# A decoder block on one core: the split weights of both feed-forwards and of four projections each at their own place modulo 128 bytes

## The chip, the core and the metric

The kernel runs on one core of a Trainium2 chip. The metric is device time in microseconds for one execution; the times below are medians over several executions. "PE" is TensorE's matmul, "PEld" its weight load, "DVE" VectorE, "ACT" ScalarE, "POOL" GpSimd, "SP" SyncE, whose queue issues most loads. One partition of the on-chip memory holds a row of bytes; all 128 partitions of a tile start at the same byte. Places below are that start byte modulo 128.

## The reference

Two layers on 512 tokens of width 1024, all in float32. Layer 0 has a dilated attention mixer, layer 1 an mLSTM mixer; behind each mixer stands a SwiGLU feed-forward with 2816 hidden units.

```python
def swiglu(xn, w_in, w_out):
    gu = xn @ w_in
    return (jax.nn.silu(gu[..., :D_FF]) * gu[..., D_FF:]) @ w_out

h = x
for i in range(2):
    if i == 0:
        h = h + dilated_attention_mixer(rms_norm(h, attn_norm[0]), positions, attn_w_in[0], attn_w_out[0])
    else:
        h = h + mlstm_mixer(rms_norm(h, mlstm_norm[0]), mlstm_w_in[0], ...)
    h = h + swiglu(rms_norm(h, ffn_norm[i]), ffn_w_in[i], ffn_w_out[i])
return rms_norm(h, final_norm)
```

## The kernel before

Every large product is done as three matmuls on float32r operands. A float32 operand is split into a high part, which ScalarE copies out in float32r, and a low part, the difference, which VectorE forms. `SPLITS` (line 46) then takes high by high, high by low and low by high, all summed in one PSUM bank. So each pair of 128-row pieces costs three matmuls, and each matmul has its own 128 by 128 weight load (the operand that stays in the array) and its own stream (the operand that moves, 512 or 256 columns).

`split_chunk` (line 231) makes the two parts of a weight chunk: a high and a low tile of 128 by 1024 float32r from the pool "w" (`wp`), each with three buffers used in turn. Four 128-row pieces of a chunk serve 12 matmuls for each of two groups of 128 outputs, thus 24 matmuls per chunk.

The stages, in the order of the program, with the matmuls that the change touches:

- Attention, up to 429 us: products at lines 541, 1059 and 1343 and projections at lines 275 and 360. Their weights come through `split_chunk` too.
- `awo`, the output projection of the attention, eight chunks through `multiply` (line 275), stream 512 wide. One of its chunks lies in a spare pool.
- Feed-forward 0 (`ffn_in`, line 1508): eight plain chunks `f0j0`, `f0j2` (line 275, 512 wide), then nine steps of seven products (a Strassen-Winograd scheme over halves of the tokens and of the width), line 1681, 24 matmuls each, 256 wide. The weight chunks are named `f0j4A11`, `f0j4S1` and so on. The stream is the split activations in tiles `op0` to `op13` of the pool "ffn0". Then the output products at line 1996, whose weights are named `f0P1_0w` and so on.
- mLSTM: `mqk` and `mo` (line 275, 512 wide), `mv` (lines 329 and 360), the heads, and the output projection `mwo` (line 275).
- Feed-forward 1 as feed-forward 0, with the pool "ffn1": plain chunks `f1j0`, `f1j2`, 63 products at line 1681, and the output products at line 2411 and 2533, in which the activations (`f1P`, in "ffn1") are what stays in the array and the weights are what moves.

The places are set by the order in which pools are opened and by the sizes of their tiles (lines 88 to 107):

```python
xp = pool(ctx, "act")
gap0 = pool(ctx, "gap0")
wp = pool(ctx, "w")
gap1 = pool(ctx, "gap1")
gap0.tile([P, 16], F32, name="gap0")
gap1.tile([P, 112], F32, name="gap1")
```

`gap0` puts 64 bytes ahead of the weights. All tiles of "w" then start at byte 96 modulo 128; the activation tiles in "act" and the operand tiles of "ffn0" and "ffn1" start at 32. A piece of a tile (256 columns, 128 weights) starts a multiple of 128 bytes further on. So in the chunks at lines 275, 1059, 1681 and 1996 the weights stand at 96 and the stream at 32, 64 bytes apart, and at lines 329, 360, 1343 and 2411 it is the other way round (stays at 32, moves at 96).

The tile framework orders the instructions by the dependencies of the buffers; nothing of that order depends on an address.

Of the kernel before, what the change touches and what calls it, by code (L numbers as in the profile page):

```python
# [3 lines left out]

# [7 lines left out]
F32 = mybir.dt.float32  # L12
F32R = mybir.dt.float32r
# [4 lines left out]
P = 128  # L18
# [3 lines left out]
KC = D // P  # L22
# [20 lines left out]
           (19, 20, 21))  # L43
LAST_OUTPUTS = {6: 22, 7: 23}
W_BUFS = 3
SPLITS = [(0, 0), (0, 1), (1, 0)]


# [27 lines left out]
def tile_hybrid_dilated_attn_mlstm(  # L76
# [8 lines left out]
    def pool(stack, name, **kw):  # L85
        return stack.enter_context(tc.tile_pool(name=name, bufs=1, **kw))

    cp = pool(ctx, "const")
    xp = pool(ctx, "act")
    gap0 = pool(ctx, "gap0")  # L90
    wp = pool(ctx, "w")
    gap1 = pool(ctx, "gap1")
    ps = pool(ctx, "psum", space=bass.MemoryType.PSUM)


# [7 lines left out]
    ones_r = cp.tile([P, P], F32R, name="ones_r")  # L103
    nc.vector.tensor_copy(ones_r, ones.to_broadcast([P, P]))

    gap0.tile([P, 16], F32, name="gap0")
    gap1.tile([P, 112], F32, name="gap1")
    idle_w = xp.tile([P, 2, SEQ], F32R, tag="x%d" % (KC - 1), name="idle_w")[:, 0]
    nc.vector.tensor_copy(idle_w, ones.to_broadcast([P, SEQ]))
    idle_ps = ps.tile([P, 512], F32, tag="t", name="idle", bufs=1)  # L110
# [94 lines left out]
    def load_chunk(src, shape, name):  # L205
        n = int(np.prod(shape[1:]))
        view = lambda t: t[:, :n].rearrange("p (a b) -> p a b", a=shape[1])
        raw = wp.tile([P, 1024], F32, tag="wraw", name=name + "_w", bufs=W_BUFS)
        nc.sync.dma_start(view(raw), src)
# [5 lines left out]
    def behind_scores():  # L215
        return tc.issue_after(ahead_of_splits[0]) if ahead_of_splits[0] is not None else nullcontext()
# [3 lines left out]
    def behind_factors():  # L220
        return tc.issue_after(ahead_of_casts[0]) if ahead_of_casts[0] is not None else nullcontext()
# [4 lines left out]
    def run_late(_):  # L226
        while lows:
            with tc.issue_after(last_on(mybir.EngineType.DVE)):
                lows.pop(0)()

    def split_chunk(chunk):

        raw, n, view, name = chunk
        p, more, bufs = (spare[0], "4", 1) if spare and next(splits) % (W_BUFS + 1) == W_BUFS else (wp, "", W_BUFS)
        hi = p.tile([P, 1024], F32R, tag="whi" + more, name=name + "_h", bufs=bufs)
        lo = p.tile([P, 1024], F32R, tag="wlo" + more, name=name + "_l", bufs=bufs)
        with behind_factors():
            nc.scalar.activation(hi[:, :n], raw[:, :n], AF.Copy)  # L238
        def low():
            nc.vector.tensor_tensor(lo[:, :n], raw[:, :n], hi[:, :n].bitcast(F32), op=ALU.subtract)  # L240
        if late[0]:
            lows.append(low)
        else:
            with behind_scores():
                low()
        return view(hi), view(lo)
# [23 lines left out]
    def multiply(acc, whl, pairs, ch, m, nk, ks=None):  # L270

        for k in ks or range(min(4, nk - 4 * ch)):
            kk = 4 * ch + k
            for a, b in SPLITS:
                nc.tensor.matmul(  # L275
                    acc, whl[a][:, k, m * P:(m + 1) * P], pairs[b][kk],
                    start=(kk == 0 and (a, b) == SPLITS[0]),
                    stop=(kk == nk - 1 and (a, b) == SPLITS[-1]))

# [39 lines left out]
    def project_tokens(pairs, w2d, c0, evac, name, tok=lambda t, tb: t[:, tb * P:(tb + 1) * P]):  # L319

        acc = [acc_tile("%s_%d" % (name, m)) for m in range(2)]
        for ch in range(KC // 4):
            whl = split_chunk(weight_chunk(w2d, ch, c0, 4, "%s_k%d" % (name, ch)))
            for m in range(2):
                with fenced():
                    for i, k in itertools.product(range(2), range(4)):
                        kk = ch * 4 + k
                        for a, b in SPLITS:
                            nc.tensor.matmul(
                                acc[m][:, i * 256:(i + 1) * 256],  # L330
                                tok(pairs[a][kk], 2 * m + i), whl[b][:, k, :],
                                start=(kk == 0 and i == 0 and (a, b) == SPLITS[0]),
                                stop=(kk == KC - 1 and (a, b) == SPLITS[-1]),
                                skip_group_check=True)
# [5 lines left out]
    def wide_chunk(parts, ch, name):  # L340
        w = 512 // len(parts)
        raw = wp.tile([P, 1024], F32, tag="wraw", name="%s_k%d_w" % (name, ch), bufs=W_BUFS)
        for i, part in enumerate(parts):
# [80 lines left out]
    with ExitStack() as actx:  # L424
# [22 lines left out]
        ang, n, sn, cs = (tmp[:, 0, i * P:(i + 1) * P] for i in range(4))  # L447
# [36 lines left out]
        xtok = ap.tile([P, TB, D], F32, tag="heads", name="x_tok")  # L484
        raws = [wp.tile([P, 1024], F32, tag="wraw", name="first%d_w" % i, bufs=W_BUFS) for i in range(2)]
        piece = lambda t, q: t[q // 2][:, (q % 2) * 512:(q % 2 + 1) * 512]
# [32 lines left out]
            else:  # L519
                nc.scalar.activation(h[k], xps[k], AF.Copy)  # L520

        his = [wp.tile([P, 1024], F32R, tag="whi", name="first%d_h" % i, bufs=W_BUFS) for i in range(2)]
        los = [wp.tile([P, 1024], F32R, tag="wlo", name="first%d_l" % i, bufs=W_BUFS) for i in range(2)]
        facc = [ps.tile([P, 512], F32, tag="o", name="a0g0q_%d" % m, bufs=2) for m in range(2)]

        def v12_parts(pr):
# [953 lines left out]
    def norm(key, k0, name, ssum=None, wait=1):  # L1480
        pair = x_tiles(name)
        add = None
        if ssum is None:
            ssum, add = squares_of(name)
        for k in range(KC):
            split_act(pair[0][k], pair[1][k], h[k], col(key, k0 + k))
            if add is not None:
                add(k)
        v = npl.tile([P, TB], F32, tag="rs_v4", name=name + "v", bufs=2)
        box = {}  # L1490

        def sums():
            sp = ps.tile([P, 512], F32, tag="t", name=name + "ss", bufs=1)
            for tb in range(TB):
                nc.tensor.matmul(sp[:, tb:tb + 1], ssum[:, tb * P:(tb + 1) * P], ones[:, 0:1],
                                 start=True, stop=True)
            nc.vector.tensor_copy(v, sp[:, :TB])
            box["finish"]()
        rbc, r, hook = inverse_rms(v, name, box)
        defer(wait, sums)  # L1500
        return pair, rbc, r, hook
# [3 lines left out]
    PLAIN = 4  # L1505
# [249 lines left out]
    def output_products(layer, fp, wo, sums_of_rows):  # L1755
# [17 lines left out]
        def subtract(out, x, y):  # L1773
            nc.vector.tensor_tensor(out, x, y, op=ALU.subtract)

        def split_operand(name, u, src):

            i = UNITS * (PARTS.index(name) % 3) + u
            nm = "f%d%s_%d" % (layer, name, u)
            if i < 2 * len(PRODUCTS):  # L1780
                t = fp.tile([P, 2, 2, HALF], F32R, tag="op%d" % i, name=nm)
                hi, lo = t[:, 0], t[:, 1]
            else:
                hi, lo = [fp.tile([P, 2, HALF], F32R, tag="gu0", name=nm, bufs=3) for _ in range(2)]
            nc.scalar.activation(hi, src, AF.Copy)
            subtract(lo, src, hi.bitcast(F32))
            ops[name, u] = [[t[:, k] for k in range(2)] for t in (hi, lo)]
# [18 lines left out]
        def prepare_first_sum(u, own, nm):  # L1806

            view = lambda t: t.rearrange("p (k n) -> p k n", k=2)
            hi = wp.tile([P, 1024], F32R, tag="whi", name=nm + "_h", bufs=W_BUFS)
            lo = wp.tile([P, 1024], F32R, tag="wlo", name=nm + "_l", bufs=W_BUFS)  # L1810
            for t, ks in first_sums[u]:
                nc.scalar.activation(view(hi)[:, ks], t, AF.Copy)
                subtract(view(lo)[:, ks], t, view(hi)[:, ks].bitcast(F32))
            whl["P5", u] = view(hi), view(lo)
            for t, ks in first_sums[u]:
                subtract(view(own)[:, ks], t, view(own)[:, ks])
            split_operand("P5", u, sums[u])
# [125 lines left out]
        first, second = (0, 1) if sums_of_rows else (1, 0)  # L1943
# [6 lines left out]
        for e in order:  # L1950
            name, i = e.split("_")
# [29 lines left out]
    pair, rbc, _, hook = norm("ffn", 0, "n1", ssum)  # L1981
    with ExitStack() as fctx:
        fp = pool(fctx, "ffn0")
# [60 lines left out]
    with ExitStack() as mctx:  # L2044
# [56 lines left out]
        gacc = acc_tile("gates")  # L2101

        def gates():
            gh = wp.tile([P, KC, P], F32R, tag="whi", name="gates_h", bufs=W_BUFS)
            nc.gpsimd.memset(gh.bitcast(F32), 0.0)
            for o in range(2):
                s = slice(32 * o, 32 * o + H)
                w = graw[:, :, o * H:(o + 1) * H]
                nc.scalar.activation(gh[:, :, s], w, AF.Copy)
                nc.vector.tensor_tensor(gh[:, :, 64 + 32 * o:64 + 32 * o + H], w, gh[:, :, s].bitcast(F32),  # L2110
                                        op=ALU.subtract)
            for k in range(KC):
                for b_ in range(2):
                    nc.tensor.matmul(gacc, gh[:, k, :], pair[b_][k], start=(k == 0 and b_ == 0),
                                     stop=(k == KC - 1 and b_ == 1))
# [68 lines left out]
        i = 0  # L2184
# [165 lines left out]
    pair, rbc, _, hook = norm("ffn", KC, "n3", ssum)  # L2350
    with ExitStack() as fctx:
        fp = pool(fctx, "ffn1")
        dp = pool(fctx, "scratch1", space=bass.MemoryType.DRAM)
        R = 32
        hid, operands, prepare, work = output_products(1, fp, ffn_w_out[1], False)
# [116 lines left out]
        def newton(tb):  # L2472
            v, r, a2 = fv[:, tb:tb + 1], fr[:, tb:tb + 1], fa[:, tb:tb + 1]
            nc.vector.reciprocal(r, r)
            nc.vector.tensor_scalar(a2, r, v, r, op0=ALU.mult, op1=ALU.mult)
            nc.vector.scalar_tensor_tensor(r, a2, -3.0, r, op0=ALU.add, op1=ALU.mult)
            return r
# [45 lines left out]
        for acc, tb, cs in tiles:  # L2523
# [21 lines left out]
            r = newton(tb)  # L2545
# [29 lines left out]
```

## Time and profile before

| | us |
|---|---|
| median of the runs before | 1357.64 (1357.39 to 1357.9, two runs) |
| the profiled execution, its own time | 1358.57 |
| its span, first to last instruction | 1356.8 |
| PE busy | 1340.1 |
| DVE busy | 1133.0 |
| ACT busy | 813.3 |
| the 63 products of feed-forward 0 (line 1681) | 171.38 |
| the 63 products of feed-forward 1 (line 1681) | 171.38 |
| the 420 matmuls of feed-forward 1's output at line 2411 | 95.97 |

A row of the chain of waits reads: start in us, length in us, engine, output, line, number of instructions. A length divided by the number of matmuls is the pace from one start to the next. That is what counts here: a single matmul's duration is longer than the pace, since consecutive matmuls overlap. A row of the windows reads: stretch, its length, busy time and count by engine, granted clock of TensorE, DMA share, GB/s; a window with a line's filter counts the instructions of that line alone.

### The profile page before, as it was taken

What the parts mean: (1) busy time and instruction counts of PE and PEld (TensorE: products, weight loads), DVE (VectorE), ACT (ScalarE), POOL (GpSimd) and SP (SyncE); (2) the same over time, 40 slices, a digit from 0 to 9 for tenths busy, and PEclk for the clock granted to TensorE, in tenths of its full rate; (3) what the DMA queues carried; (4) which work ended last, traced back from release to release, by engine and by line L of the source; (5) the groups of instructions that cost most, each with busy time, mean ns of one, the idle gap of its engine ahead of it and who ended that gap; (6) DMA issues with size and microseconds to landing.
All of it is one profiled execution on the core that took longest, in us unless ns stands there. A gap on an engine that the chain in (4) does not pass through costs nothing.

```text
span 1356.8 us, 23343 instructions
## 1 busy us (share of the span) xinstructions
PE 1340.1 (99%) x9100; PEld 1222.1 (90%) x9100; DVE 1133.0 (84%) x1787; ACT 813.3 (60%) x1303; POOL 196.7 (14%) x272
## 2 busy tenths in 40 slices
PE   9999999999999999999999999999999999999997
PEld 7898899999988888999999998898878899999886
DVE  7988789899876389888888898898848988997887
ACT  6676577667674255555577464795534555558854
POOL 3000013141412001000010110122200112112113
PEclk9999999999999999999999999999999999999999
DMA  9354244554676357343362743324333545447863
GB/s 306 122 181 155 79 141 143 169 172 155 184 261 191 125 142 172 114 125 125 125 156 79 171 126 87 100 63 124 94 118 97 127 133 172 141 136 173 189 171 101
DMA packets 141270, 194.90 MB, mean 144 GB/s; under 512 B 9028, under 2 KB 106116, under 8 KB 141160
## 3 DMA queue, kind: packets, MB, share of 16 engines
q1 hardware_dynamic: 120128, 140.73, 33.0%
q0 software_dynamic: 19808, 52.48, 16.1%
q8 instruction: 71, 1.16, 0.3%
q10 hardware_dynamic: 1224, 0.21, 0.1%
q14 instruction: 39, 0.32, 0.1%
HBM read 167.30 MB, written 22.54 MB: 140 GB/s over the span
## 4 chain that ended last, share of the span: by engine, by line
PE 79%; DVE 10%; ACT 3%; issue 3%; DMA 1%; POOL 0%; SPq 0%; ACTq 0%; DVEq 0%; POOLq 0%
PE fo L1996 7%; PE f1j_u L1681 5%; PE f0j_u L1681 5%; PE f1j_c L1681 4%; PE f0j_c L1681 4%; PE f1j_p L1681 4%; PE f0j_p L1681 4%; PE mwo L275 3%; PE f1j L275 3%; PE f0j L275 3%; PE mqk L275 3%; PE awo L275 3%; PE finp L2411 3%; PE mo L275 3%; PE finc L2411 2%
## 5 line engine op out<-in xcount | busy, mean ns | idle before, releaser
L1803 POOL DMA_DIRECT2D f0S<-in_ffn_w_out_dram x10 | 8.7, 874 | 248.9 <-DVE f0hid L1720 162.3
L2364 POOL DMA_DIRECT2D hD<-hB x32 | 20.7, 655 | 109.6 <-DVE hB L2361 109.4
L1828 POOL DMA_DIRECT2D f1T<-in_ffn_w_out_dram x15 | 17.8, 1186 | 86.1 <-ACT f1T L1831 40.8
L240 DVE TENSOR_TENSOR v1P_l<-v1W,v1P_h 128x1024 fp32r<-128x1024 f32 x14 | 17.1, 1224 | 10.3 <-ACT v1P_h L238 10.3
L275 PE MATMUL mo<-n_h,mo_k_h 128*128 128x512 f32 x64 | 25.7, 401 | 0.0
L275 PE MATMUL mwo<-yo_h,mwo_k_h 128*128 128x512 f32 x64 | 25.5, 398 | 0.0
L275 PE MATMUL awo<-ao_h,awo_k_h 128*128 128x512 f32 x64 | 25.5, 398 | 0.0
L275 PE MATMUL mwo<-yo_l,mwo_k_h 128*128 128x512 f32 x64 | 25.5, 398 | 0.0
L275 PE MATMUL mwo<-yo_h,mwo_k_l 128*128 128x512 f32 x64 | 25.5, 398 | 0.0
L275 PE MATMUL mo<-n_h,mo_k_l 128*128 128x512 f32 x64 | 25.4, 397 | 0.0
L275 PE MATMUL mqk<-n_h,mqk_k_h 128*128 128x512 f32 x64 | 25.4, 397 | 0.0
L275 PE MATMUL mo<-n_l,mo_k_h 128*128 128x512 f32 x64 | 25.4, 396 | 0.0
L275 PE MATMUL mqk<-n_l,mqk_k_h 128*128 128x512 f32 x64 | 25.3, 396 | 0.0
L275 PE MATMUL awo<-ao_l,awo_k_h 128*128 128x512 f32 x64 | 25.3, 396 | 0.0
L275 PE MATMUL f0j<-n_h,f0j_h 128*128 128x512 f32 x64 | 25.3, 395 | 0.0
L275 PE MATMUL f1j<-n_h,f1j_h 128*128 128x512 f32 x64 | 25.3, 395 | 0.0
L275 PE MATMUL awo<-ao_h,awo_k_l 128*128 128x512 f32 x64 | 25.3, 395 | 0.0
L275 PE MATMUL mqk<-n_h,mqk_k_l 128*128 128x512 f32 x64 | 25.2, 394 | 0.0
L275 PE MATMUL f0j<-n_l,f0j_h 128*128 128x512 f32 x64 | 25.2, 394 | 0.0
L275 PE MATMUL f1j<-n_l,f1j_h 128*128 128x512 f32 x64 | 25.2, 394 | 0.0
L275 PE MATMUL f0j<-n_h,f0j_l 128*128 128x512 f32 x64 | 25.2, 394 | 0.0
L275 PE MATMUL f1j<-n_h,f1j_l 128*128 128x512 f32 x64 | 25.2, 394 | 0.0
(2746 smaller groups left out, 5999.6 us busy)
## 6 DMA issues: line engine op xcount, KB each, us to landing
f0j_w<-in_ffn_w_in_dram SPq DMA_DIRECT2D x17, 512.0 KB, 5.7
f1j_w<-in_ffn_w_in_dram SPq DMA_DIRECT2D x17, 512.0 KB, 6.9
f1T<-in_ffn_w_out_dram POOLq DMA_DIRECT2D x15, 512.0 KB, 6.4
f0hid<-in_ffn_w_in_dram SPq DMA_DIRECT2D x9, 512.0 KB, 6.1
f1hid<-in_ffn_w_in_dram SPq DMA_DIRECT2D x9, 512.0 KB, 5.0
v0W<-in_attn_w_in_dram SPq DMA_DIRECT2D x8, 512.0 KB, 6.8
v1W<-in_attn_w_in_dram SPq DMA_DIRECT2D x8, 512.0 KB, 3.7
awo_k_w<-in_attn_w_out_dram SPq DMA_DIRECT2D x8, 512.0 KB, 4.7
```

The source lines that it names most:

```text
L240: nc.vector.tensor_tensor(lo[:, :n], raw[:, :n], hi[:, :n].bitcast(F32), op=ALU.subtract)
L275: nc.tensor.matmul(acc, whl[a][:, k, m * P:(m + 1) * P], pairs[b][kk], start=(kk == 0 and (a, b) == SPLITS[0]), stop=(kk == nk - 1 and (a, ...
L1681: nc.tensor.matmul(acc[name][:, m * HALF:(m + 1) * HALF], whl[a][:, k, m * P:(m + 1) * P], ops[okey][b][:, k], start=(fresh and m == 0 and ...
L1803: nc.gpsimd.dma_start(t, src[1][:, ks], accum_op=ALU.add)
L1828: nc.gpsimd.dma_start(view(to), weight_rows(hk * UNITS + u, n), accum_op=ALU.add)
L1996: nc.tensor.matmul(acc, w[a_][:, k, m * P:(m + 1) * P], b[b_][k], start=(fresh and k == 0 and (a_, b_) == SPLITS[0]), stop=(k == 1 and (a_ ...
L2364: nc.gpsimd.dma_start(hD[k // 4].rearrange("(b i) x -> i b x", i=R)[:, :, c0:c0 + R], t[R * a_:R * (a_ + 1)])
L2411: nc.tensor.matmul(acc[m], a[a_][k][:, (2 * t + m) * P:(2 * t + m + 1) * P], w[b_][:, k, :], start=(fresh and k == 0 and (a_, b_) == SPLIT ...
```

## The change

The two gap pools go. The high and low tiles of "w" become 1056 columns wide (`PAD` is 32 columns, 128 bytes) and only 1024 of them are used, from a column that `place_of` gives by the chunk's name. The pool "w" now begins at byte 32, so column 16, which most names get, is byte 96 as before. For the products' weights of both feed-forwards the column goes up by 5 (20 bytes) from chunk to chunk, modulo 32; for the plain chunks by 10 (40 bytes); for `awo`, `mqk`, `mo` and `mwo` by 5. Over a feed-forward's 63 products every multiple of 4 bytes is used once or twice. A tile of 32 bytes ahead of the others in "ffn1" moves everything in that pool from 32 to 64 modulo 128: the stream of feed-forward 1's products, and the staying operand of line 2411.

Both high and low tile of a chunk get the same column, so a place holds for 24 matmuls. On every engine the instructions, their shapes and their waits stand in the same order as before; only addresses differ. The weights at lines 541, 1059, 1343, 329, 360 and 1996 keep byte 96; raw tiles of "w", which SP's queue fills, go from 96 to 32.

```diff
+PAD = 32
...
-    gap0 = pool(ctx, "gap0")
     wp = pool(ctx, "w")
-    gap1 = pool(ctx, "gap1")
...
+    products = ("A11", "S1", "S2", "A12", "S3", "S4", "A22")
+
+    def place_of(name):
+
+        i, found = None, re.match(r"f([01])j(\d+)([AS]\d+)$", name)
+        if found:
+            i = int(found[1]) * 66 + (int(found[2]) - PLAIN) // 2 * 7 + products.index(found[3])
+            return (i * 5 - 8) % PAD
+        found = re.match(r"f([01])j(\d)_(\d)(\d)$", name)
+        if found:
+            i = int(found[1]) * 8 + int(found[2]) * 2 + int(found[3]) * 2 + int(found[4])
+            return (i * 10 - 8) % PAD
+        found = re.match(r"(awo|mqk|mo|mwo)(\d)_k(\d)$", name)
+        if found:
+            i = ("awo", "mqk", "mo", "mwo").index(found[1]) * 8 + int(found[3]) * 4 + int(found[2])
+            return (i * 5 - 8) % PAD
+        return 16
+
     def split_chunk(chunk):
 
         raw, n, view, name = chunk
         p, more, bufs = (spare[0], "4", 1) if spare and next(splits) % (W_BUFS + 1) == W_BUFS else (wp, "", W_BUFS)
-        hi = p.tile([P, 1024], F32R, tag="whi" + more, name=name + "_h", bufs=bufs)
-        lo = p.tile([P, 1024], F32R, tag="wlo" + more, name=name + "_l", bufs=bufs)
+        at, pad = (0, 0) if more else (place_of(name), PAD)
+        hi = p.tile([P, 1024 + pad], F32R, tag="whi" + more, name=name + "_h", bufs=bufs)[:, at:at + 1024]
+        lo = p.tile([P, 1024 + pad], F32R, tag="wlo" + more, name=name + "_l", bufs=bufs)[:, at:at + 1024]
...
         fp = pool(fctx, "ffn1")
+        fp.tile([P, 8], F32, name="gap3")
```

The three other places that take tiles of "w" (the first projection, the first sums of feed-forward 0's output, the gates) get 1056 columns and column 16.

More of the change, by code (lines that the diff above doesn't have):

```diff
@@ L2 @@
 import math
+import re
 from contextlib import ExitStack, nullcontext
@@ L104, in tile_hybrid_dilated_attn_mlstm @@
     nc.vector.tensor_copy(ones_r, ones.to_broadcast([P, P]))
-    gap0.tile([P, 16], F32, name="gap0")
-    gap1.tile([P, 112], F32, name="gap1")
     idle_w = xp.tile([P, 2, SEQ], F32R, tag="x%d" % (KC - 1), name="idle_w")[:, 0]
@@ L520, in x_keep @@
                 nc.scalar.activation(h[k], xps[k], AF.Copy)
-        his = [wp.tile([P, 1024], F32R, tag="whi", name="first%d_h" % i, bufs=W_BUFS) for i in range(2)]
-        los = [wp.tile([P, 1024], F32R, tag="wlo", name="first%d_l" % i, bufs=W_BUFS) for i in range(2)]
+        his = [wp.tile([P, 1024 + PAD], F32R, tag="whi", name="first%d_h" % i, bufs=W_BUFS)[:, 16:1040] for i in range(2)]
+        los = [wp.tile([P, 1024 + PAD], F32R, tag="wlo", name="first%d_l" % i, bufs=W_BUFS)[:, 16:1040] for i in range(2)]
         facc = [ps.tile([P, 512], F32, tag="o", name="a0g0q_%d" % m, bufs=2) for m in range(2)]
@@ L1808, in prepare_first_sum @@
             view = lambda t: t.rearrange("p (k n) -> p k n", k=2)
-            hi = wp.tile([P, 1024], F32R, tag="whi", name=nm + "_h", bufs=W_BUFS)
-            lo = wp.tile([P, 1024], F32R, tag="wlo", name=nm + "_l", bufs=W_BUFS)
+            hi = wp.tile([P, 1024 + PAD], F32R, tag="whi", name=nm + "_h", bufs=W_BUFS)[:, 16:1040]
+            lo = wp.tile([P, 1024 + PAD], F32R, tag="wlo", name=nm + "_l", bufs=W_BUFS)[:, 16:1040]
             for t, ks in first_sums[u]:
@@ L2103, in gates @@
         def gates():
-            gh = wp.tile([P, KC, P], F32R, tag="whi", name="gates_h", bufs=W_BUFS)
+            gh = wp.tile([P, 1024 + PAD], F32R, tag="whi", name="gates_h", bufs=W_BUFS)[:, 16:1040]
+            gh = gh.rearrange("p (k n) -> p k n", k=KC)
             nc.gpsimd.memset(gh.bitcast(F32), 0.0)
```

## The prediction

> **What bounds the kernel now.** I read the page first, for its busy times and the clock.
>
> ```profile
> span 1356.8 us, 23343 instructions
> PE 1340.1 (99%) x9100; PEld 1222.1 (90%) x9100; DVE 1133.0 (84%) x1787; ACT 813.3 (60%) x1303; POOL 196.7 (14%) x272
> PEclk9999999999999999999999999999999999999999
> PE 79%; DVE 10%; ACT 3%; issue 3%; DMA 1%; POOL 0%; SPq 0%; ACTq 0%; DVEq 0%; POOLq 0%
> ```
>
> TensorE has work 99% of the time at an undiminished clock, and 79% of the chain that ends last is its matmuls. Nothing but the pace of the matmuls, from one start to the next, can move the time much. The windows show the two stretches that the change touches most, the products of the feed-forwards, first with all engines (PE, PEld, DVE, ACT, POOL, clock, DMA), then line 1681 alone.
>
> ```profile
> 526.78:698.16 171.38, 171.38 (x1515) 171.38 (x1514) 149.40 (x150) 97.30 (x123) 3.89 (x4) 1.00 0.44 130
> 526.78:698.16 171.38, 171.38 (x1512) 171.18 (x1511) 1.00 0.44 130
> 1070.47:1241.85 171.38, 171.38 (x1512) 171.18 (x1511) 1.00 0.46 144
> ```
>
> No gap in either: 1512 matmuls in 171.38 us, 113.35 ns each, with the weight load busy all the time as well. VectorE is busy for 149.40 us of it and so has 22 us in hand. Then the chain, for the pace of other stretches of the same shapes.
>
> ```profile
> 86.52 2.72 PE a0g2c L1059 x24
> 92.15 2.83 PE a0g2p L1059 x24
> 97.80 5.60 PE v0c L1343 x24
> 398.35 11.00 PE a3g12v L360 x48
> 495.99 30.80 PE f0j L275 x132
> 529.52 2.72 PE f0j_p L1681 x24
> 832.93 22.39 PE mqk L275 x96
> 862.37 5.66 PE mv L329 x48
> ```
>
> Here is what the argument rests on. Streams 256 wide have at least two paces: 2.72/24 = 113.3 ns and 2.83/24 = 117.9 ns (line 1059; line 329 gives 5.66/48 = 117.9 too). Streams 512 wide have at least two: 5.60/24 = 233.3 (also 30.80/132 and 22.39/96) and 11.00/48 = 229.2. In the program all of these have the weights and the stream 64 bytes apart modulo 128. So the pace isn't given by the shape alone, nor by the places alone: at equal places the rows at 86.52 and 92.15 differ. Between them lies a matmul that waited; a rhythm, once entered, goes on. In feed-forward 0 and 1 all 126 products run in the faster of the two.
>
> **The change part by part.** No instruction, shape or wait changes, so what is removed and added costs nothing by itself. Four things get other addresses.
>
> *Weights of the 126 products: 3024 matmuls.* Each product has its own distance between weights and stream, by steps of 4 bytes over all 32. The trace has no steady 256-wide stretch at another distance than 64, so this cost is bounded. Above: all products in the slower rhythm, 117.9 - 113.35 = 4.55 ns x 3024 = 13.8 us. [...]
>
> ```profile
> 264.78 1.61 PE L902 MATMUL a0o<-a0pT,a0v 128*128 128x128 f32 x13
> L902 PE MATMUL a0o<-a0pT,a0v x32: 275/275/275, 264.6 to 275.0; 128*128 128x128 f32 x32
> ```
>
> Thirteen matmuls take 1.61 us, the last of them 0.275 us; (1.61 - 0.275)/12 = 111.3 ns, half the columns for nearly the same pace. So the gain is at most 2.05 x 3024 = 6.2 us. I take two products in five in the slower rhythm, 0.4 x 13.8 = +5.5 us: the present distance holds the faster rhythm in all 126, a new one every 2.72 us gives many occasions to leave it, and a rhythm left is not regained by itself. That share is my choice, not a reading.
>
> [...]
>
> *Weights of the plain chunks and four projections.* 48 chunks, of which one of `awo` lies in the spare pool, so 47 x 24 = 1128 matmuls, now at 233.3 ns, the slower of the two 512-wide rhythms. The one burst whose weights and stream start at the same byte (32 and 32, the last matmuls) is in the timeline:
>
> ```profile
> 1339.20 0.39 PE L2533 MATMUL finc<-f1w_h,f1hh 128*128 128x512 f32 x1
> ...
> 1340.34 0.39 PE L2533 MATMUL finc<-f1w_h,f1hl 128*128 128x512 f32 x1
> 1340.56 0.40 PE L2533 MATMUL finp<-f1P_3w_h,f1P 128*128 128x512 f32 x1
> ```
>
> Six matmuls from 1339.20 to 1340.56, 226.7 ns each. So the bounds are 6.6 x 1128 = 7.4 us of gain and, as 233.3 is already the slowest long stretch that I find, no loss below the rival that follows. I take 231, between 229.2 and 233.3, since other distances mix the rhythms and the 226.7 stands in six matmuls alone: 2.3 x 1128 = -2.6 us.
>
> *Feed-forward 1's pool 32 bytes on.* It moves the stream of 1512 of the products, which is in the first term, and the staying operand of line 2411, whose distance goes from 64 to 96:
>
> ```profile
> 1241.85:1337.82 95.97, 95.97 (x420) 78.53 (x419) 1.00 0.74 162
> ```
>
> 95.97/420 = 228.5 ns. Bounds 226.7 and 233.3: -0.8 to +2.0 us; I take 1 ns, +0.4 us, nearer to its present pace than to the slower.
>
> *VectorE and ScalarE* now write and read these tiles off a multiple of 16 bytes.
>
> ```profile
> L240 DVE TENSOR_TENSOR f0j14A_l<-f0j14A,f0j14A_h 128x1024 fp32r<-128x1024 f32 x2 | 2.5, 1227 | 0.9 <-ACT f0j14A_h L238 0.9
> L2073 DVE SCALAR_TENSOR_TENSOR conv<-pre,cols,conv x24: 715/746/983, 846.0 to 908.5; 128x512 f32<-128x512 f32 x24
> ```
>
> The convolution at line 2073 reads at 4, 8 and 12 bytes past its tile's start, and its 24 instructions lie near 746 ns, one excepted: no price by offset. What hides a small one: the 63 subtractions of 1.227 us per feed-forward would have to lengthen by 22/63 = 0.35 us, 28%, before VectorE has no time in hand. Taken at 0; without that cover every further 0.1 us would be 63 x 0.1 = 6.3 us per feed-forward. SP's loads now land at byte 32 instead of 96, with DMA at 0.44 of its share: 0 as well.
>
> Sum: 5.5 - 2.6 + 0.4 = +3.3 us. The profiled execution took 1358.57 (span 1356.8 and 1.8 around it) and becomes 1361.9; the median shown, 1357.64, lies 0.9 below it, so 1360.9, say 1361. With all bounds low it is -6.2 - 7.4 - 0.8 = -14.4, 1343; with all high 13.8 + 2.0 = +15.8, 1373.
>
> **The rivals.**
>
> *Distance doesn't matter.* Every stretch keeps the rhythm that it is in: 1357.6, plus or minus 2. For it: distance 64 occurs with both rhythms, and what separates them is a wait before. [...] Against it: the burst at equal bytes is the fastest 512-wide stretch of the trace. Chance 0.20.
>
> *Most new distances are better.* The weight chunks fall to 229 or below and the products to between 113.35 and 111.3: 1343 to 1353. For it: 512-wide streams run in their slowest rhythm now, at the one distance tried. Against: the largest term, the products, has only 2 ns above its floor. Chance 0.20. Faster by over 2% (27 us) it can't be by rows, whose floor is 1343. [...] I leave it 0.02 of the 0.20.
>
> *Weight load and stream collide at most distances* (slower than before). Twice a 256-wide pace is 226.7 and the plain chunks take 233.3, so something costs 6.6 ns per weight load there. If each weight load in a product paid two of these, 13.2 ns, at three places in four, that is 0.75 x 3024 x 13.2 = 30 us and the chunks stay as they are: 1388, 2.2% slower. It decides from 27/3024 = 9 ns more per matmul on average, a product of 2.93 us. For it: weight load and stream are both busy all the time in the products, so every place where they clash is paid. Against: the longest regular 256-wide rhythm in the trace is only 4.55 ns over the present one. Chance 0.08; between my forecast and it, at 1373 to 1385, another 0.07.
>
> That the change doesn't do what it says I don't count: the places follow from the names and the pool sizes.
>
> **How the numbers follow.** Forecast, a mix of rhythms between 1353 and 1373: 0.45. The chances are 0.45 + 0.20 + 0.20 + 0.07 + 0.08. The time is that of the mix, 1361. The range, 1345 to 1378, holds the mix, the no-effect case, nearly all of the better case and half of what lies between 1373 and 1385; about 0.15 is outside. A measurement of this kernel tells about 2%, 27 us, from no change: faster 0.02, same 0.90, slower 0.08.
>
> **What would show it.** In the chain the pieces "f0j_p L1681 x24" and their kin should no longer all be 2.72 us: some 2.83, in runs that follow each other. If all stay at 2.72, the no-effect rival holds; if the length follows the place (the same place giving the same length in both passes over the 32), then distance and not history sets the rhythm; pieces of 2.9 us and more are the collision. The chunks should show 5.44 to 5.60 us per 24 instead of 5.60 throughout. VectorE's subtractions should stay near 1.23 us, and PE busy should have no gaps in the products; gaps that end at VectorE or ScalarE would prove the fourth part wrong. The forecast is wrong if the products' windows together grow by over 14 us or shrink at all.

## The result

The changed kernel takes 1372.81 us (two runs, 1372.72 and 1372.89), the kernel before 1357.64: a ratio of 1.0111, 95% interval 1.0089 to 1.0133. The prediction was 1361, range 1345 to 1378: inside the range, slower as forecast, and 12 us above the point. The first rows of the page after, busy times and chain:

```profile
span 1371.1 us, 23343 instructions
PE 1353.3 (99%) x9100; PEld 1234.3 (90%) x9100; DVE 1133.7 (83%) x1787; ACT 813.9 (59%) x1303; POOL 196.6 (14%) x272
PEclk9999999999999999999999999999999999999999
PE 79%; DVE 10%; ACT 3%; issue 3%; DMA 1%; POOL 0%; SPq 0%; DVEq 0%; ACTq 0%; POOLq 0%
```

The span grew by 14.3 us and TensorE's busy time by 13.2, while VectorE and ScalarE grew by less than 1 us each and the clock stayed whole. So the same 9100 matmuls run at a slower pace, and the chain is TensorE's to the same 79%. Where, the windows say; first feed-forward 0's products with all engines, then line 1698 (1681 before) alone in both feed-forwards, then line 2430 (2411 before) alone, with the same columns as in the prediction:

```profile
524.75:703.50 178.75, 178.75 (x1515) 178.75 (x1514) 149.74 (x150) 97.28 (x123) 3.95 (x5) 1.00 0.42 124
524.75:703.50 178.75, 178.75 (x1512) 178.54 (x1511) 1.00 0.42 124
1075.49:1254.34 178.85, 178.85 (x1512) 178.65 (x1511) 1.00 0.45 138
1254.34:1352.29 97.95, 97.95 (x420) 78.51 (x419) 1.00 0.74 159
```

Still no gap; VectorE's 149.74 us is what it was. But 1512 matmuls take 178.75 and 178.85 us in place of 171.38: 118.2 and 118.3 ns each, together +14.84 us. Line 2430 takes 97.95 us where the prediction's window had 95.97; counted from its first start to the start after its last matmul, it is +1.8 us. In the chain of waits after, the pieces that answer to those of the prediction:

```profile
108.10 5.54 PE v0c L1360 x24
494.06 30.70 PE f0j L292 x132
524.75 2.85 PE f0j_c L1698 x24
527.60 2.83 PE f0j_p L1698 x24
550.35 2.94 PE f0j_u L1698 x24
838.15 22.32 PE mqk L292 x96
```

Every product shown is at 2.83 us or more; 2.94, a product at distance 20, is the longest of them (the other product at 20 in feed-forward 0 took 2.84). The chunks (f0j and mqk in line 292, 275 before) went from 30.80 to 30.70 and from 22.39 to 22.32, all 1200 matmuls of line 292 together to 1.1 us less. Line 1360 (1343 before) has 5.54 where it had 5.60, though nothing of its distance changed. The few products that ran at the fast pace aren't among the pieces above; the windows of single products show one, with its neighbours:

```profile
590.17:593.00 2.83, 2.83 (x26) 2.83 (x26) 1.00 0.00 0
593.00:595.73 2.73, 2.73 (x26) 2.73 (x26) 1.00 0.00 0
595.73:598.62 2.89, 2.89 (x26) 2.89 (x26) 1.00 0.55 157
```

The middle one is the product whose weights stand 64 bytes from the stream (44 before it, 84 after; the windows also count a neighbour's matmul at each end). It goes to 2.73 us at once and the next one leaves again. So I sorted the starts of all product matmuls by distance: three or four products for each, mean ns from start to start in the changed kernel, and behind the stroke in the sweep of the experiments:

```
  0 119.1/118.8    4 117.9/118.8    8 117.6/118.1   12 117.4/117.2
 16 118.3/118.4   20 119.7/118.4   24 118.9/118.7   28 119.5/119.4
 32 119.0/118.5   36 118.4/117.9   40 119.1/119.4   44 118.3/118.3
 48 118.7/119.0   52 116.9/116.1   56 118.5/118.3   60 119.0/119.0
 64 114.1/113.5   68 118.1/118.1   72 119.1/119.1   76 114.5/113.6
 80 118.3/117.7   84 119.0/119.9   88 116.6/118.1   92 119.2/119.0
 96 117.9/118.0  100 118.9/119.0  104 119.4/118.7  108 118.8/118.9
112 118.2/117.7  116 118.0/118.7  120 118.3/118.8  124 118.8/119.3
```

### The profile page after: what moved, and what is told of

Read it like the earlier page. It is cut to its first block, busy times and chain, and to the rows that moved or that the text cites. A ratio compares the mean times of both kernels' runs of the same rounds, so it can differ in the third digit from the quotient of the medians.

```text
span 1371.1 us, 23343 instructions
## 1 busy us (share of the span) xinstructions
PE 1353.3 (99%) x9100; PEld 1234.3 (90%) x9100; DVE 1133.7 (83%) x1787; ACT 813.9 (59%) x1303; POOL 196.6 (14%) x272
## 4 chain that ended last, share of the span: by engine, by line
PE 79%; DVE 10%; ACT 3%; issue 3%; DMA 1%; POOL 0%; SPq 0%; DVEq 0%; ACTq 0%; POOLq 0%
PE fo L2013 6%; PE f0j_u L1698 6%; PE f1j_u L1698 6%; PE f1j_c L1698 4%; PE f0j_p L1698 4%; PE f1j_p L1698 4%; PE f0j_c L1698 4%; PE mwo L292 3%; PE f1j L292 3%; PE f0j L292 3%; PE awo L292 3%; PE mo L292 3%; PE mqk L292 3%; PE finp L2430 3%; PE finc L2430 2%
```

## The experiments

Two theories. *Distance*: the bytes between weights and stream modulo 128 decide whether a 256-wide sequence can run at 113.3 ns; 64 can, nearly all others can't. *History*: the step from place to place throws the sequence out of its rhythm, whatever the place. A third reading is that other byte offsets, the wider tiles or the moved pool cost time as such. The edits below are to the changed kernel unless they say otherwise; "chunks" are the plain chunks and four projections.

### One constant distance, 64 and then 0

The three lines place the products, the plain chunks and the projections.

```diff
-            return (i * 5 - 8) % PAD
+            return (16, 24)[int(found[1])]
-            return (i * 10 - 8) % PAD
+            return 7
-            return (i * 5 - 8) % PAD
+            return 7
```

> The changed kernel, but every product of both feed-forwards has its weights 64 bytes from its stream modulo 128 (place 16 in feed-forward 0, place 24 in feed-forward 1, whose stream stays 32 bytes on), and every plain chunk and projection has them at distance 28. Distance theory: the products go back to 113.3 ns each and 342.7 us in all, though in feed-forward 1 both weights and stream lie at other bytes than before; the whole is 1372.8 - 14.9 = 1358 us, and 1351 to 1358 if the chunks take up to the 6 ns less at distance 28 that single ones of them showed. Theory that the new byte offsets, the wider tiles or the moved pool cost the time as such: feed-forward 1 stays at about 118 ns, the whole stays above 1364.

The other has (0, 8), 0 and 0 at these places.

> The changed kernel, but every product has its weights at distance 0 from its stream in both feed-forwards, and every plain chunk and projection too, so that nothing moves from one product to the next. Distance theory: 117.5 to 119.5 ns a matmul in the products, 355 to 361 us in all (342.7 before), the whole at 1370 to 1376 us as with the change. History theory (it is the step from place to place that throws the products out of the fast rhythm): 113.3 ns throughout, the whole at about 1358. For the 512-wide chunks at distance 0 both leave 227 to 236 ns open.

The first takes 1357.77 us, ratio 1.0002 (0.9993 to 1.0012); the second 1374.00, ratio 1.0121 (1.0101 to 1.0141). The products' windows, of the kernel at 64 and of that at 0:

```profile
523.36:695.11 171.75, 171.75 (x1512) 171.35 (x1511) 1.00 0.43 129
1066.37:1237.90 171.53, 171.53 (x1512) 171.33 (x1511) 1.00 0.46 144
```

```profile
524.74:704.23 179.49, 179.49 (x1512) 179.29 (x1511) 1.00 0.41 124
1075.25:1255.46 180.21, 180.21 (x1512) 180.01 (x1511) 1.00 0.44 137
```

At 64 the whole loss is gone, though weights and stream of feed-forward 1 lie at other bytes than before and the tiles keep their 32 columns more. At 0 nothing moves from product to product, and they run at 118.7 and 119.2 ns. That ends the history theory and the third one: with the products at distance 64, offsets, widths and the pool cost them 0.5 us at most, 0.4 of it in feed-forward 0, whose weight loads are busy for 171.35 of the 171.75 us, against 171.33 of 171.53 in feed-forward 1. In the total the kernel at 64 stands level with the one before because smaller things nearly cancel: its chunks, at distance 28, are 3.3 us faster, line 2430 is 1.8 slower and the products 0.5.

### The sweep

```diff
-            return (i * 5 - 8) % PAD
+            return (i // 2 if i < 66 else 31 - (i - 66) // 2) % PAD
...
-        fp.tile([P, 8], F32, name="gap3")
```

The chunks stand at place 28.

> The changed kernel without the 32-byte gap in feed-forward 1; each distance is held for two products, rising from 0 to 124 bytes by 4 in feed-forward 0 and falling from 124 to 0 in feed-forward 1; plain chunks and projections all at distance 112. Distance theory: 113.3 to 116 ns only at about 52 to 76 bytes, 117 to 120 elsewhere, the same curve rising and falling, products about 355 us in all. History theory: the fast rhythm, once entered near 64, is kept as the distance moves on, so that rising it is fast from 64 upwards and falling from 64 downwards; the two curves differ. The chunks at distance 112 should show whether the 229 ns that a single chunk had there holds for all.

It took 1373.03 us in one run. The falling half in its chain of waits, two pieces for each distance, from 80 down to 48:

```profile
1142.32 2.85 PE f1j_u L1698 x24
1145.17 2.73 PE f1j_c L1698 x24
1147.90 2.72 PE f1j_u L1698 x24
1150.62 2.84 PE f1j_p L1698 x24
...
1159.17 2.84 PE f1j_p L1698 x24
1162.01 2.73 PE f1j_u L1698 x24
1164.73 2.72 PE f1j_c L1698 x24
1167.46 2.88 PE f1j_u L1698 x24
...
1178.83 2.74 PE f1j_p L1698 x24
1181.58 2.72 PE f1j_u L1698 x24
1184.30 2.83 PE f1j_c L1698 x24
```

Fast pairs stand at 76, 64 and 52, and nowhere else; between them, at 72, 68, 60 and 56, the sequence is back at 2.83 to 2.88. In the rising half the pairs at 64 and 76 are fast, 5.45 us each, and the one at 52, 5.69 us, isn't. So my expectation of a fast stretch from 52 to 76 was wrong in form: it is three single distances, 12 bytes apart. And the fast rhythm isn't kept when the distance moves on: behind 2.72 us come 2.84, 2.88 and 2.83. Two products per distance can miss one, though: at 88, another 12 bytes on, the sweep shows 117 to 120 ns, while in the changed kernel one of the four products at 88 (at 1200.31 us) ran at 114.0. No run holds 88 for a whole stretch, so whether it is a fourth fast distance stays open. The chunks at 112 ran at 231.8 ns on average: the single chunk at 229 didn't speak for them.

### 76 and 52 held

Products at place 19 in feed-forward 0 and 13 in feed-forward 1, chunks at 6, no gap.

> No gap; every product of feed-forward 0 at distance 76, every one of feed-forward 1 at distance 52; plain chunks and projections at distance 24. If the fast distances are single ones 12 bytes apart, as the sweep suggests: feed-forward 0 at 113.5 ns, +0.2 us; feed-forward 1 at 113.4 to 114.2, up to +1.3 us, or, since two products at 52 were fast in the falling half of the sweep and two slow in the rising half, 118 throughout and +7.5 us if the rhythm that it starts in stays. If only 64 is fast and 76 and 52 owed it to a neighbour: 118 in both, +7.5 us each.

It took 1356.77 us in one run. The two windows, then the start of feed-forward 0 in the chain:

```profile
524.81:696.33 171.52, 171.52 (x1512) 171.32 (x1511) 1.00 0.43 129
1067.43:1239.05 171.62, 171.62 (x1512) 171.42 (x1511) 1.00 0.46 143
```

```profile
524.82 2.84 PE f0j_c L1698 x24
527.65 2.76 PE f0j_p L1698 x24
530.41 2.72 PE f0j_u L1698 x24
```

Both distances hold the fast pace, 113.4 and 113.5 ns over the windows. They begin in the slow rhythm and slide out of it, at 76 within two products, at 52 within three (118.0, 118.3, 114.3 ns, then 113.3). Two products can thus be too few for 52, which fits the slow pair in the rising half of the sweep. What made the pair in the falling half fast at once isn't shown.

### One tile of two at the fast distance

```diff
         hi = p.tile([P, 1024 + pad], F32R, tag="whi" + more, name=name + "_h", bufs=bufs)[:, at:at + 1024]
+        at = 16 - at if re.match(r"f[01]j\d+[AS]\d+$", name) else at
         lo = p.tile([P, 1024 + pad], F32R, tag="wlo" + more, name=name + "_l", bufs=bufs)[:, at:at + 1024]
```

Products at place 16 in feed-forward 0 and 0 in feed-forward 1, chunks at 12, no gap.

> No gap; within each product the two tiles of weights differ: in feed-forward 0 the high parts (two matmuls of three) lie at distance 64 and the low parts (one of three) at 0, in feed-forward 1 the other way round; plain chunks and projections at distance 48. If each matmul pays by its own distance: (2 x 113.3 + 118.9)/3 = 115.2 ns in feed-forward 0 and (113.3 + 2 x 119.2)/3 = 117.2 in feed-forward 1, +2.8 and +5.8 us. If the fast pace is a rhythm of the whole sequence that one off-beat load in three breaks: about 118 to 119 in both, +7 to +8.6 us each. Chunks at 48: 230.5 ns if the two chunks that stood there with the change speak for all.

It took 1372.04 us in one run.

```profile
525.24:703.86 178.62, 178.62 (x1512) 178.42 (x1511) 1.00 0.41 124
1075.19:1254.39 179.20, 179.20 (x1512) 179.00 (x1511) 1.00 0.44 137
```

These windows of its products give 118.1 and 118.5 ns, and 115.2 was the price of paying matmul by matmul. With one load in three at distance 0 none of the three matmuls keeps the fast pace: sorted by their place among the three, the matmuls of feed-forward 0 are 117.9, 118.8 and 117.7 ns apart on average. The chunks at 48 ran at 231.1.

### Each part alone

The kernel before, with nothing but the pool's 32 bytes:

```diff
         fp = pool(fctx, "ffn1")
+        fp.tile([P, 8], F32, name="gap3")
```

> The kernel before with one part of the change alone: the pool of feed-forward 1 lies 32 bytes on, so that its 1512 product matmuls stand at a constant distance of 32 bytes and line 2411 at 96. Distance theory: feed-forward 1's products at 117.5 to 120 ns, +6.3 to +10 us, line 2411 at 233 ns as with the whole change, +1.8 us; 1365.5 to 1369.5 in all, while feed-forward 0 stays at 113.3 ns. History theory (nothing moves within the products): only the +1.8 of line 2411, 1359.5.

And the changed kernel without that line:

> The other part of the change alone: the weights move, feed-forward 1's pool stays. Distance theory: feed-forward 1's products still meet all distances, 118.2 ns and +7.3 us as in the sweep; feed-forward 0 +7.3; chunks -1.1, line 2411 +0.9: 1357.2 + 14.4 = 1371.6, 1370.5 to 1373. So the pool's 32 bytes, which cost 9.7 us alone, add about 1 us to the moved weights. If the parts added up: 1372.8 - 9.7 = 1363.

The gap alone takes 1366.88 us, ratio 1.0065 (1.0048 to 1.0081), the weights alone 1372.25, ratio 1.0116 (1.0101 to 1.0132). The windows of the products and of line 2412 with the gap alone:

```profile
526.93:698.29 171.36, 171.36 (x1512) 171.17 (x1511) 1.00 0.43 130
1070.46:1249.37 178.91, 178.91 (x1512) 178.72 (x1511) 1.00 0.44 138
1249.37:1347.37 98.00, 98.00 (x420) 78.38 (x419) 1.00 0.74 158
```

Feed-forward 1 at a constant 32 runs at 118.3 ns in all 63 products, +7.5 us, and line 2412 at 96 is 1.9 slower. With the weights alone feed-forward 1 takes 178.94 us (7.6 more), because there too nearly every product is off its distance. So the parts don't add: 9.7 and 15.6 alone make 15.2 together. Feed-forward 1's products take 178.91 us with the gap alone, 178.94 with the weights alone and 178.85 with both.

### Looking for a faster kernel

Products at 64, no gap, all chunks at 28, and the 512-wide lines whose stream is the split chunk (1343, 360, 2411) at 28 as well:

```diff
+        if re.match(r"v\d+.*_\d$|a\dg12v_k\d$|f1P\d_\dw$", name):
+            return 25
         return 16
```

> No gap in feed-forward 1; all products at distance 64, which the sweep showed fast; plain chunks and projections at distance 28, and also the 512-wide lines 1343 (336 matmuls), 360 (168 of its 288) and 2411 (396 of its 420), which stood at 64 before. Distance theory: products at 342.7 us as before, chunks 3.3 us below before as in the run with all products at 64, and the three lines lose up to 2.2, 0.7 and 0.9 us: 1350.3 to 1354.3 against 1357.4, a ratio of 0.995 to 0.998. Theory that the pace of 512-wide streams doesn't hang on the distance: no line moves by more than 0.5 us, ratio 1.000.

This failed: 1361.68 us, ratio 1.003 (1.0018 to 1.0042), slower than before.

```profile
1241.54:1340.90 99.36, 99.36 (x420) 79.54 (x419) 1.00 0.73 156
```

Line 2431 (2411 before), shown here, lost 3.2 us where 0.9 of gain was hoped for; lines 1343 and 360 lost 1.2 and 1.4. The chunks at 28 gained 1.8 us here and not 3.3: 19 of the 48 ran at 226.7 ns or close to it, against 26 in the kernel with all products at 64, and others at up to 239. Distance 28, at which the chunks, whose weights are the split tile, gained, costs the lines whose stream it is: line 2431 takes 99.36/420 = 236.6 ns there, against 228.9 in the kernel before. The next two look further; the first with chunks at 24 and the attention's split weights at 76,

```diff
+        if re.match(r"a\dg\dP\d$", name):
+            return 19
```

> Meant to beat both: no gap; products at 64; plain chunks and projections at distance 24, where all of them ran at 230 to 232 ns; the attention's split weights (1488 matmuls of line 1059) at 76, where the products left the slow rhythm after one to two products, while at 64 about 24 groups of 24 keep it through whole stretches. Distance theory: chunks -1.9 us, line 1059 up to 24 x 24 x 4.55 = -2.6 us, line 2411 +0.9 and line 360 +0.4 as in the other runs without the gap, line 1343 -0.7: 1353 to 1356.5 against 1357.2, ratio 0.997 to 0.9995. If what a wait leaves behind, and not the distance, decides in the short stretches of the attention, line 1059 stays at 221 us: 1356 to 1357.

the second with the attention's at 52 and a distance of its own for every group of 12 in lines 1343 and 2411:

```diff
+        if re.match(r"v\d+.*_\d$|f1P\d_\dw$", name):
+            swept.append(name)
+            return (16 + len(swept)) % PAD
```

> No gap; products at 64, plain chunks at 24; attention's split weights at 52; in the 512-wide lines 1343 and 2411 every group of 12 matmuls stands at the next distance, 4 bytes from the one before, through all 32. If the pace of 512-wide streams follows the distance at once: each group of 12 between 226.7 and 237 ns, with the groups near 28 at 235 to 237 and single ones at 226.7 to 229. If it needs longer than 12 matmuls to settle: all near 231 to 233. Line 1059 at 52: as at 76, up to 2.6 us less than 221.6, or as before.

The first took 1356.28 us, ratio 0.9992 (0.998 to 1.0004), no difference. Its chunks gained 2.0 us. In line 1059, the groups whose median start-to-start time is over 116 ns fell from 23 to 4, and yet the line is only 0.4 us shorter: its starts up to 140 ns apart add up to 207.5 us before and 205.8 here, the longer ones, which hold a wait, to 14.1 and 15.4. So the waits took most of it. Nor is the fall shown to be due to distance 76. In the changed kernel, where the line stands at 64 in the wider tiles, 7 such groups are left. In the kernel with the gap alone, whose attention is that of the kernel before, there are 31, and the line takes 222.3 us against 221.6. The wider tiles, then, go with most of the fall, and 0.4 us is less than two equal attentions differ by. The second took 1357.66 us in one run, its line 1059, at 52, staying at 221.8 with 16 such groups. Its sweep of line 2436 (2411 before) in the chain, distances 16, 12, 8, 4, 0, 124, 120, 116:

```profile
1281.21 2.72 PE finu L2436 x12
1283.94 2.85 PE finp L2436 x12
1286.78 2.81 PE finu L2436 x12
1289.59 2.74 PE finp L2436 x12
1292.34 2.80 PE finu L2436 x12
1295.14 2.85 PE finp L2436 x12
1297.98 2.81 PE finu L2436 x12
1300.79 2.78 PE finp L2436 x12
```

Here the pace follows the distance at once, and modulo 16: 12 and 124 cost 2.85 us (237 ns), 4 and 116 take 2.74 and 2.78, 0, 8 and 120 lie between, and the one exception is 16, the fastest with 2.72 (226.7). The whole line says the same: its groups at 12 modulo 16 took 234 to 238 ns, those at 4 modulo 16 228 to 232. The last two kernels put lines 1343, 2411 and 360 at 16, with chunks at 24 and at 28:

> The kernel with chunks at 24 and the attention's weights at 76, and now the 512-wide lines whose stream is the split chunk at distance 16: 1343 (336 matmuls), 2411 (396 of 420) and 360 (168 of 288). If the 226.7 ns that single groups of 12 showed there in the sweep holds for the whole lines: 1343 at 76.2 us (78.4 before), 2411 at 95.2 (96.1), 360 about 66; with the chunks' -2.0 and the attention's -0.4 the whole comes to 1351 to 1353.5 against 1356.9, ratio 0.995 to 0.998. If a group's place in the sequence made those groups fast: the lines stay at 231 to 233 ns, ratio 0.999 to 1.000.

> The same with the plain chunks and projections at distance 28 in place of 24. Chunks held 28 with -3.3 us in one kernel and -1.8 in another; here -1.8 to -3.3 against -2.0 at 24: from 1.3 us better than the kernel at 24 to 0.2 worse, the other lines alike. If the two differ by more, it is what the chunks leave behind for the stretches after them.

With chunks at 24: 1356.10 us, ratio 0.999 (0.9981 to 0.9998); at 28: 1354.70, ratio 0.9982 (0.9973 to 0.9991). The hoped-for 226.7 held in one group of three, as the chain of the kernel with chunks at 24 shows in line 2433 (2411 before):

```profile
1252.64 2.78 PE finp L2433 x12
1255.43 2.72 PE finc L2433 x12
1258.15 2.82 PE finp L2433 x12
```

2.78, 2.72, 2.82 in turn, and so on: the split tiles lie in three buffers taken in turn, 4224 bytes apart. In the kernel before they lie 4096 apart and the line has one pace, 2.75. That it goes with the buffers and not with distance 16 shows in the kernel of 1356.28 us further up, which has the wider tiles but keeps this line (2431 there) at 64:

```profile
1252.54 2.75 PE finp L2431 x12
1255.29 2.76 PE finc L2431 x12
1258.05 2.81 PE finp L2431 x12
```

So for this line the distance modulo 128 isn't all, and line 1343 gained 1.1 us, line 2411 lost 1.0. Distance 16 is the smaller part of both: at 64 in the wider tiles, line 1343 had already gained 0.6 and line 2411 lost 0.9. The chunks at 28 gained 3.7 us, the largest single gain; a long piece of theirs in the chain before and in the last kernel:

```profile
985.40 38.92 PE mwo L275 x166
```

```profile
981.70 37.95 PE mwo L296 x166
```

That kernel, with products at 64, chunks at 28, the attention's weights at 76 and lines 1343, 360 and 2411 at 16, is the fastest of all, 2.7 us under the one before; the one with chunks at 24 is faster by 1.3, hardly more than its interval.

## Why the prediction was right and wrong

**The total.** 1372.81 us lies within the range because the range is wide, and at the slow edge of the forecast mix (1353 to 1373). The three terms of the sum all came out slower than taken, by 9.3, 1.5 and 1.4 us; together they make the 12 us. So the direction was right, but the time stayed in the range by luck more than by the mechanism.

**The bound.** Right: TensorE's pace, at a clock of 1.00 throughout, made all the difference.

**Products, forecast +5.5 us, measured +14.8.** This is the step that failed: "I take two products in five in the slower rhythm". It rested on three reasons. "The present distance holds the faster rhythm in all 126" held. "A new one every 2.72 us gives many occasions to leave it" named the wrong cause: constant distances of 0 and 32 are as slow as moving ones. "A rhythm left is not regained by itself" is wrong for these stretches: a product at 64 regains it at once (2.73 us, behind 2.83), and held distances of 76 and 52 within two or three products. In place of the share stands a property of the distance: 64, 76 and 52 are fast when held, 0 and 32 are slow when held, and the others, seen for one or two products at a time, are slow on average. By the upper price, 4.55 ns, all products would have made 13.8 us; the measured mean was 4.9 ns, as most distances lie at 118 to 119.5 and not at the 117.9 of the rows. So the upper bound, too, was 1 us low. The lower one took 111.3 ns, the pace of matmuls of 128 columns, as the least for 256; no run shows that it is, and the fastest window of 63 products, 171.36 us, has 113.3. The prediction's own test, growth of over 14 us, speaks against the mixed rhythm, and its other one, length by place and not by history, is what came.

**The reading behind it.** "Nor by the places alone" was read rightly from two paces at one distance: a wait can leave a sequence at 64 in the slow rhythm. In the trace before, the weight load of line 1059 at 89.29 us starts 0.21 us behind the one ahead of it, where those before it start 0.11 apart; the line's matmuls run 113 ns apart up to there and 118 behind it. I then let that stand for all distances. It says only that 64 allows both; what the other distances allow, no row could say.

**Chunks, forecast -2.6, measured -1.1.** Direction right, size less than half: on average over all distances they run about 1 ns faster per matmul than at 64, not 2.3. The fastest pace I had from six matmuls, 226.7, is real, and at 28 a good half of the chunks (26 of 48) have it. But it isn't the pace of equal places: the six matmuls just before those six, with the same operands at the same bytes, take 230.8 ns in the same trace, which the prediction left out, and the chunks held at distance 0 ran at 231.2 on average.

**Line 2411, forecast +0.4, measured +1.8.** Within its bounds, near the upper one: 233.2 ns at distance 96, as in the kernel with the gap alone (98.00 us). The sum overlooked that the wider tiles alone cost this line 0.9 us at 64 (97.05 with the weights alone); the two don't add.

**VectorE, ScalarE, the loads, forecast 0.** Right; the subtraction that the prediction quoted takes 1226 ns in place of 1227:

```profile
L257 DVE TENSOR_TENSOR f0j14A_l<-f0j14A,f0j14A_h 128x1024 fp32r<-128x1024 f32 x2 | 2.5, 1226 | 1.5 <-ACT f0j14A_h L255 1.5
```

**Left out of the sum.** The wider tiles put the three buffers 4224 bytes apart. With them line 1343, whose distance stayed at 64, took 0.6 us less. Line 360 took 0.4 more, but with the gap alone, where its tiles are as before, it took 0.3 more as well, so that isn't shown to come from the tiles.

**The rivals.** No effect is out: the gap alone costs 9.7 us. In the kernel with the gap alone only an address changes, and the same matmuls take 118.3 in place of 113.3 ns. What they lose those 5 ns to, no record shows. Better at most distances is out for the products and holds only a little for the chunks. The collision came nearest in the pattern, a price at nearly all distances, but of 4.9 ns and not 9.9 on average, so 1373 and not 1388; that loads and streams collide isn't shown.

What the runs leave open is why it is 52, 64 and 76, and whether a distance that no run held for longer, 88 above all, belongs to them. The traces have starts and durations, and none shows what a load or a stream reads.

## What to carry over

Where TensorE is hardly ever idle (99% busy here), the place of the weights against the stream inside a partition is a parameter like any other: here 4.3% of a 256-wide float32r matmul's pace hangs on it (118.2 against 113.35 ns), so keep the distance that works when a pool or a tile is resized, or sweep it within one run, a distance for each group, and read the windows by distance. Hold each candidate over a whole stretch before believing it, since single groups at 229 and 226.7 ns didn't hold (231.8 for the chunks, and 226.7 in one group of three for line 2411). And two edits that lead into the same slow rhythm didn't add here, 9.7 and 15.6 us making 15.2: try each alone.

## What was not expected of the hardware

- 256-wide float32r matmuls, each with its own weight load, ran at 113.3 to 113.6 ns over the 63 products of a feed-forward at distances of 64, 76 and 52 bytes modulo 128 when these were held. Held at 0 and 32 they took 118.3 to 119.2 ns; at the other distances, seen for one or two products at a time, 116.6 to 120 on average. With one load in three at distance 0 they took 118.1.
- At distance 64 both rhythms occur: 2.72 and 2.83 us for 24 matmuls of line 1059, the slow one from a weight load on that came 0.1 us late, at 89.29 us.
- 512-wide streams ran between 226.7 and 239 ns. In line 2411, whose stream is the split tile, one run shows 234 to 238 ns for the groups at 12 modulo 16 and 228 to 232 for those at 4; with the buffers 4224 bytes apart, the groups of 12 take 2.75, 2.76 and 2.81 us in turn at distance 64, and 2.78, 2.72 and 2.82 at 16. In the chunks, whose weights it is, 28 gave 226.7 to 26 of 48 (19 in another kernel) and up to 239 to others, and 0, 24, 48 and 112 gave 231 to 232 on average.
- With split tiles off a multiple of 16 bytes, the subtraction of a chunk took 1226 ns in place of 1227, and VectorE and ScalarE in all 1133.7 and 813.9 us in place of 1133.0 and 813.3.
